# Products with w_pb in a hybrid decoder layer taken to Strassen's recursion, with tiles of w_pa between its pairs

## The chip, the cores and the metric

The kernel runs on one core of a Trainium2 chip. The metric is the device time of one execution in microseconds (us). Engines: TensorE (PE) multiplies matrices, VectorE (DVE), ScalarE (ACT) and GpSimd (POOL) do the element-wise work, SyncE (SP) issues most loads. Each engine runs its instructions in order; semaphores order them against one another.

## What is computed

One decoder layer, in float32, on 576 tokens (512 of a prompt and 64 of a sample), with model width 1024:

```python
h      = x @ w_in          # u | v | q | k | v | gate_A | gate_B
y_A    = u * (tril(W_s[g]) v_chunk + b_s[g])          # chunked spatial gating
y_B    = sliding-window attention with sinks
m      = (sigmoid(gate_A) * (y_A @ w_pa) + sigmoid(gate_B) * (y_B @ w_pb)) @ w_o
x      = LN1(alpha * x + m);  x = LN2(alpha * x + SwiGLU(x))
```

The change concerns the gates (16 column tiles of w_in, 128 columns each), y_A @ w_pa and y_B @ w_pb (8 column tiles each).

## The kernel before

**Numbers.** Every float32 operand is split into a high part (a cast on ScalarE, line 115) and a low part (a subtraction on VectorE, line 116). A product is three matmuls: high by high, high by low, low by high. Weights come as units of 512 KB in the order in which the host packed them (`_weights`). `fetch` loads a unit into one of three `raw` buffers, `convert` splits it into `hi` and `lo` (four buffers each). Names ending in h or hi, l or lo are the two parts.

**Two ways to multiply.** `fm` takes one column tile of 128 weights: 8 pieces of the inner dimension by 2 halves of the tokens (288 each) by 3, so 48 matmuls. `pair` takes two column tiles at once by Strassen's recursion in Winograd's form: seven products (B11, T1, T2, B22, B21, T3, T4) of 12 matmuls, 84 instead of 96, into three PSUM banks x, y, z, whose contents are added in the output tiles g and u on VectorE (line 225) or copied there by ScalarE (lines 228, 231, 238). Its weights are sums of the quarters of two units, made in `weight_group`: "sums" (two subtractions on VectorE, one on GpSimd), "1" (split of B11 and T1), "2" (T3 and T2, from the tile t), "3" (B22, B21, and a subtraction on GpSimd), "4" (T4). While a pair multiplies, the next pair's weights are made; a pair's last product T4 runs inside the next pair, after its T1. The left operands need sums of the quarters of the activations: for the input x these are S1, S2, S4 (`input_sums`, made during the products of v, acc_v, from loads xr) and S3 (`input_sum3`, made at the start of the gates from four more loads xs and written over a part of X).

**Stages around the change.** acc_v (v, ends at 259.0 us); seven gate pairs (to 359.3), during which steps of other work, the list `todo` (layer norm of v, key outputs, spatial gate, splits of y_A), are taken up at two spots of each pair; eight w_pa tiles by `fm`, whose results are multiplied by sigmoid(gate) (`times`, line 987); eight w_pb tiles by `fm`, each followed by `times`, an addition on GpSimd (line 1003) and a split of the sum into the stacked operand m (`stacked`, lines 1010 to 1013); the output projection acc_o. The feed-forward part after it uses `pair` throughout.

**What sets the order.** Inside a `manual_schedule` the engines' order is the program's order; elsewhere a scheduler chooses it from modelled costs. SG is a pool of four buffers of 128x576, C and R are pools of larger tiles that are handed on when their last reader is done.

Of the kernel before, what the change touches and what calls it, by code (L numbers as in the profile page):

```python
# [18 lines left out]
P = 128  # L19
# [58 lines left out]
class Builder:  # L78
# [135 lines left out]
    def pair(self, name, left, g, u, first, final, more):  # L214
# [8 lines left out]
        nxt = self.weight_group() if more else self.units_ahead()  # L223
# [5 lines left out]
        self.spare(0)  # L229
        go(z, "T1")  # L230
        nc.scalar.copy(out=u[:, hi], in_=z)
        nxt["1"]()
        if rest:
            rest()
        w["4"]()
        self.spare(2)
        go(x, "T2", False)
        nc.scalar.copy(out=u[:, lo], in_=x)
        self.spare(3)
        go(z, "B22", False)  # L240
        add(u, lo, z)
        go(y, "B21")
        add(g, lo, y)
        first()
        nxt["3"]()
        go(x, "T3", False)
        add(u, hi, x)
        nxt["2"]()

        def finish():  # L250
            go(x, "T4", False)
            final(x)

        self.rest, self.w = finish, nxt
# [5 lines left out]
    @staticmethod  # L260
    def left(x, S):

        out = {
            "B11": lambda c: (x[:, c, :HB], x[:, c, NT : NT + HB]),
            "B21": lambda c: (x[:, 4 + c, :HB], x[:, 4 + c, NT : NT + HB]),
            "T4": lambda c: (x[:, 4 + c, HB:NT], x[:, 4 + c, NT + HB :]),
        }
        for n, (hi, lo) in zip(("T1", "T2", "T3", "B22"), S):
            out[n] = lambda c, hi=hi, lo=lo: (hi[:, c], lo[:, c])
        return out  # L270
# [619 lines left out]
    def input_sums(self):  # L890

        nc = self.nc
        S = [[self.C([4, HB], F32R, f"X{n}{i}") for i in "hl"] for n in ("S1", "S2", "S4")]
        tt = lambda e, out, x, y, op: e.tensor_tensor(out=out, in0=x, in1=y, op=op)
        for c in range(4):
            p, q = self.SG(f"xr{c}"), self.SG(f"xr{c + 4}")
            nc.sync.dma_start(out=p[:], in_=self.I["xT"][:, c])
            nc.sync.dma_start(out=q[:], in_=self.I["xT"][:, c + 4])
            a11, a21, a12, a22 = p[:, :HB], p[:, HB:], q[:, :HB], q[:, HB:]
            tt(nc.gpsimd, a22, a21, a22, ALU.add)  # L900
            tt(nc.vector, a11, a22, a11, ALU.subtract)
            tt(nc.vector, a12, a12, a11, ALU.subtract)
            for (hi, lo), a in zip(S, (a22, a11, a12)):
                self.split(hi[:, c], lo[:, c], a)
        self.XSums = S

    def input_sum3(self):

        nc = self.nc
# [27 lines left out]
    def merge(self):  # L937
# [22 lines left out]
        self.todo.insert(4, self.key_outputs)  # L960
# [16 lines left out]
        for g in range(len(yA), 8):  # L977
            part(yA, self.u[g // 2][:, g % 2], self.C, f"yA{g}")

        def product(j, name, y):  # L980
            ps = [self.bank(f"ps{name}{j}_{b}") for b in range(2)]
            self.fm(ps, self.unit(KC), lambda k: (y[k][:, 0], y[k][:, 1]))
            return ps

        def times(ps, x, out):
            for b, t0, t1 in HALVES:
                nc.vector.tensor_tensor(out=out[:, t0:t1], in0=ps[b][:, :HB], in1=x[:, t0:t1], op=ALU.mult)

        for j in range(8):
            ps = product(j, "pa", yA)  # L990
            with self.tc.issue_after(self.last_split.ins):
                times(ps, T[j], T[j])
# [3 lines left out]
        for j in range(8):  # L996
            part(yB, self.yB[j // 2][:, j % 2], self.C, f"yBs{j}")
        self.m = []
        for j in range(8):
# [98 lines left out]
    def ffn(self):  # L1098
# [26 lines left out]
        self.spots = (3,)  # L1125
# [135 lines left out]
def _weights(w_in, w_pa, w_pb, w_o, w_gate, w_up, w_down):  # L1261
# [30 lines left out]
    for w in (w_pa, w_pb):  # L1292
        for j in range(8):
            fm(w[:, P * j : P * j + P])
# [70 lines left out]
```

## Time and profile before

| | |
|---|---|
| three runs | 909.65, 911.98 and 2240.95 us, median 911.98 |
| profiled execution | 911.2 us, span 909.5 |
| TensorE busy | 886.5 us, 97% of the span |
| VectorE, ScalarE, GpSimd busy | 608.1, 388.5, 164.5 us |
| granted TensorE clock | 0.991 on average |

A share of the span is an average over stages. Where an engine that is busy 97% of the time waits, its waits are few and can be listed one by one, each with the instruction that ended it. The line numbers in the profile are those of the kernel before; a helper's line (283 for every matmul, 115 and 116 for every split) stands for many places, so the tile's name tells which one is meant, with buffer numbers left out.

### The profile page before, as it was taken

Reading aid. Unit: us, or ns where it says so; the run is one execution under the profiler, and the core shown is the slowest. Engines: PE = TensorE matmul, PEld = TensorE weight load, DVE = VectorE, ACT = ScalarE, POOL = GpSimd, SP = SyncE. Lnnn points to the kernel's source line nnn. Section 1 sums busy time; section 2 is a strip of 40 time slices with the busy share of each in tenths; the row PEclk is TensorE's granted clock in tenths of the full one; section 3 lists DMA queues with packets and bytes.
Section 4 is the critical chain, followed back from the end, with each engine's and each line's share of the span. In section 5 each row is a group of like instructions: output and inputs, shape, how many; then the busy total and the mean of one; then the engine's idle time right before and its main releaser. Section 6 shows DMA issues by size and latency. Waiting matters only on the chain.

```text
span 909.5 us, 14732 instructions
## 1 busy us (share of the span) xinstructions
PE 886.5 (97%) x5963; PEld 830.5 (91%) x5963; DVE 608.1 (67%) x893; ACT 388.5 (43%) x739; POOL 164.5 (18%) x190
## 2 busy tenths in 40 slices
PE   9799999999998999999999999999999999999996
PEld 7799999997888999999988999999999998888885
DVE  4578977865677779245657877777777779315146
ACT  4456665566245447122231444444444457211110
POOL 1003123332242210002201222222222210000003
PEclk9899999999999999999999999999999999999998
DMA  7731212426131324444261012233222225322202
GB/s 210 209 102 47 71 48 75 157 94 221 47 108 63 111 94 138 155 131 140 74 227 47 1 50 91 97 100 99 98 94 95 93 94 157 101 90 82 81 1 105
DMA packets 33101, 93.16 MB, mean 102 GB/s; under 512 B 4039, under 2 KB 11095, under 8 KB 33001
## 3 DMA queue, kind: packets, MB, share of 16 engines
q1 hardware_dynamic: 32840, 90.04, 30.7%
q10 hardware_dynamic: 192, 2.18, 0.6%
q8 instruction: 47, 0.77, 0.3%
q14 instruction: 22, 0.17, 0.1%
HBM read 88.08 MB, written 6.10 MB: 104 GB/s over the span
## 4 chain that ended last, share of the span: by engine, by line
PE 78%; DVE 11%; ACT 5%; DMA 3%; issue 2%; POOL 1%; SPq 0%; POOLq 0%; ACTq 0%; DVEq 0%
PE d L283 15%; PE xf L283 14%; PE zf L283 7%; PE acc_o L283 6%; PE pspb L283 6%; PE pspa L283 6%; PE acc_v L283 5%; PE xg L283 4%; PE yf L283 3%; DMA raw<-in_wall_dram 3%; PE ffn L283 3%; ACT work L563 2%; PE zg L283 2%; DVE lo L116 2%; PE psg L283 1%
## 5 line engine op out<-in xcount | busy, mean ns | idle before, releaser
L116 DVE TENSOR_TENSOR lo<-raw,hi 128x1024 fp32r<-128x1024 f32 (+1 forms) x86 | 108.6, 1271 | 106.5 <-ACT hi L115 106.1
L115 ACT CAST hi<-raw 128x1024 fp32r<-128x1024 f32 (+1 forms) x86 | 84.1, 990 | 180.1 <-PE d L283 82.6
L116 DVE TENSOR_TENSOR glo<-raw,ghi 128x1024 fp32r<-128x1024 f32 (+1 forms) x81 | 87.5, 1081 | 65.0 <-ACT ghi L115 64.5
L283 PE MATMUL d<-hi,h 128*128 128x512 f32 (+1 forms) x440 | 128.0, 368 | 0.0
L115 ACT CAST ghi<-raw 128x1024 fp32r<-128x1024 f32 (+1 forms) x81 | 72.6, 898 | 52.6 <-DVE raw L178 42.0
L283 PEld LDWEIGHTS d<-hi,h 128*128 128x128 f32 x440 | 79.8, 188 | 13.8
L283 PE MATMUL d<-lo,h 128*128 128x512 f32 (+1 forms) x242 | 89.6, 370 | 0.0
L178 POOL TENSOR_TENSOR raw<-raw,t 128x512 f32<-128x512 f32 x27 | 34.9, 1292 | 177.4 <-DVE glo L116 165.2
L283 PE MATMUL xf<-x1T,ghi 128*128 128x288 f32 x320 | 65.0, 295 | 0.0
L116 DVE TENSOR_TENSOR glo<-t,ghi 128x1024 fp32r<-128x1024 f32 x27 | 58.1, 2153 | 0.0
L178 POOL TENSOR_TENSOR t<-raw,raw 128x512 f32<-128x512 f32 x27 | 35.9, 1329 | 100.5 <-DVE raw L178 100.5
L283 PEld LDWEIGHTS d<-lo,h 128*128 128x128 f32 x242 | 45.6, 188 | 7.8
L283 PEld LDWEIGHTS xf<-x1T,ghi 128*128 128x128 f32 x320 | 51.4, 188 | 0.2 <-DVE u L225 0.2
L283 PE MATMUL xf<-x1T,glo 128*128 128x288 f32 x160 | 47.1, 294 | 0.0
L283 PE MATMUL acc_o<-hi,m 128*128 128x512 f32 x144 | 46.2, 390 | 0.0
L313 POOL TENSOR_SCALAR lnr<-lnmv 128x1 f32<-128x1 f32 (+1 forms) x15 | 13.6, 907 | 175.8 <-DVE lnmv L331 172.6
L283 PE MATMUL psu<-X,hi 128*128 128x288 f32 x256 | 44.1, 294 | 0.0
L283 PE MATMUL pspb<-yBs,hi 128*128 128x288 f32 x256 | 44.1, 293 | 0.0
L283 PE MATMUL pspa<-yA,hi 128*128 128x288 f32 x256 | 44.1, 294 | 0.0
L283 PE MATMUL acc_v<-hi,X 128*128 128x512 f32 x128 | 41.6, 391 | 0.0
L563 ACT ACTIVATE work<-work,att 128x128 f32<-128x128 f32 x64 | 25.0, 391 | 37.6 <-DVE att L560 37.6
L283 PE MATMUL psq<-X,hi 128*128 128x288 f32 x224 | 38.6, 294 | 0.0
(339 smaller groups left out, 2402.8 us busy)
## 6 DMA issues: line engine op xcount, KB each, us to landing
raw<-in_wall_dram SPq DMA_DIRECT2D x133, 512.0 KB
xr<-in_xT_dram SPq DMA_DIRECT2D x8, 288.0 KB
z<-in_xtok_dram SPq DMA_DIRECT2D x4, 512.0 KB
xraw<-in_xT_dram SPq DMA_DIRECT2D x3, 576.0 KB
out_y_prompt_dram<-z SPq DMA_DIRECT2D x3, 512.0 KB
xs<-in_xT_dram SPq DMA_DIRECT2D x4, 288.0 KB
circ<-bout SPq DMA_DIRECT2D x1, 1024.0 KB
Bsel<-circ SPq DMA_DIRECT2D x2, 512.0 KB
```

What stands on the lines that cost most here:

```text
L115: self.nc.scalar.copy(out=hi, in_=src)
L116: return self.nc.vector.tensor_tensor(out=lo, in0=src, in1=hi.bitcast(F32), op=ALU.subtract)
L178: sub = lambda e, out, x, y: e.tensor_tensor(out=out, in0=x, in1=y, op=ALU.subtract)
L283: self.last_mm = self.nc.tensor.matmul(out, l, r, start=start, stop=stop, **more)
L313: self.nc.gpsimd.tensor_scalar_add(r[:n], mv[:n, 1:2], EPS)
L563: nc.scalar.activation(out=pr[:, r], in_=sel[:, r], func=AF.Exp, bias=nm[:, r : r + 1], accum_out=rs[:, r : r + 1])
```

## The change

1. **w_pb.** The products with w_pb become four Strassen pairs (p0 to p3). Their left operands are splits of y_B (tile Y, in the buffer of X) and of its sums (SA, SB), which are made between the first w_pa tiles, partly on GpSimd. The first five w_pa tiles run plainly, the other three stand between a pair's T3 and T4. Multiplying by the gates (`final`), adding the w_pa part on GpSimd and stacking m move into the pairs. The host packs w_pb's units as sums ask for them.
2. **S3 of the input.** The difference a11 - a21 is formed on GpSimd inside `input_sums`, when the loads xr are there, and kept in two SG tiles (s3_0, s3_1) until the gates start; the loads xs go. Two of the four SG buffers are left for the eight xr tiles.
3. **Side work.** The two spots of a gate pair are now directly after the next pair's "sums" (0, 6) instead of before T2 and B22 (2, 3); `pair` takes its steps from a table `plan`.

```diff
+        if plan is None:
+            nxt = self.weight_group() if more else self.units_ahead()
+            plan = {0: (nxt["sums"],), 2: (nxt["1"],), 3: (w["4"],), 6: (nxt["3"],), 7: (nxt["2"],)}
         go = lambda out, n, first=True: self.product(out, w["ops"][n], left[n], first, True)
         add = lambda t, s, ps: nc.vector.tensor_tensor(out=t[:, s], in0=ps, in1=t[:, s], op=ALU.add)
-        nxt["sums"]()
+
+        def do(n):
+            if n in (6, 7):
+                self.spare(n)
+            for step in plan.get(n, ()):
+                step()
+            if n not in (6, 7):
+                self.spare(n)
+
+        do(0)
...
+        s3 = [self.SG(f"s3_{i}") for i in range(2)]
+        self.s3raw = [s3[c // 2][:, HB * (c % 2) : HB * (c % 2) + HB] for c in range(4)]
...
+            tt(nc.gpsimd, self.s3raw[c], a11, a21, ALU.subtract)
...
-            p = self.SG(f"xs{c}")
-            nc.sync.dma_start(out=p[:], in_=self.I["xT"][:, c])
-            nc.gpsimd.tensor_tensor(out=p[:, HB:], in0=p[:, :HB], in1=p[:, HB:], op=ALU.subtract)
-            self.split(hi[:, c], lo[:, c], p[:, HB:])
+            self.split(hi[:, c], lo[:, c], self.s3raw[c])
...
-        self.spots = (2, 3)
+        self.spots = (0, 6)
...
+        def sums(c):
+
+            p, q = (self.yB[k // 2][:, k % 2] for k in (c, c + 4))
+            self.split(Y[:, c, :HB], Y[:, c, NT : NT + HB], p[:, :HB])
+            self.split(Y[:, c + 4, :NT], Y[:, c + 4, NT:], q)
+            a11, a21, a12, a22 = p[:, :HB], p[:, HB:], q[:, :HB], q[:, HB:]
+            tt = lambda e, out, x, y, op: e.tensor_tensor(out=out, in0=x, in1=y, op=op)
+            tt(nc.gpsimd, a22, a21, a22, ALU.add)
+            tt(nc.gpsimd, a21, a11, a21, ALU.subtract)
+            tt(nc.vector, a11, a22, a11, ALU.subtract)
+            tt(nc.vector, a12, a12, a11, ALU.subtract)
+            part(SA, p, self.C, f"SA{c}")
+            part(SB, q, self.C, f"SB{c}")
...
+        plain = 5
+        for j in range(plain):
+            u = self.unit(KC, ahead=int(j + 1 < plain))
+            if j + 1 == plain:
+                self.first_pair()
+            ps = product(j, u)
             with self.tc.issue_after(self.last_split.ins):
-                times(ps, T[j], T[j])
+                times(j, ps)
+            if j < 4:
+                sums(j)
...
+        half = lambda t, s: lambda c: (t[c][:, 0, s], t[c][:, 1, s])
+        lo, hi = slice(0, HB), slice(HB, NT)
+        left = self.left(Y, (half(SB, hi), half(SA, lo), half(SA, hi), half(SB, lo)))
         self.m = []
-        for j in range(8):
-            ps = product(j, "pb", yB)
-            with self.tc.issue_after(self.last_split.ins):
-                times(ps, gB[j], gB[j])
-            nc.gpsimd.tensor_tensor(out=gB[j][:], in0=gB[j][:], in1=T[j], op=ALU.add)
-            self.m.append(self.stacked(gB[j], f"m{j}"))
+        stack = lambda: self.m.append(self.stacked(gB[len(self.m)], f"m{len(self.m)}"))
+
+        def pairs(i):
+
+            j = 2 * i
+            r = self.C([2, NT], F32, f"pb{i}")
+            g, u = r[:, 0], r[:, 1]
+            ga, gb = gB[j], gB[j + 1]
+            mul = lambda out, x, y: nc.vector.tensor_tensor(out=out, in0=x, in1=y, op=ALU.mult)
+
+            def final(x):
+                mul(ga[:, hi], x, ga[:, hi])
+                mul(gb[:], u, gb[:])
+                for k, t in ((j, ga), (j + 1, gb)):
+                    nc.gpsimd.tensor_tensor(out=t[:], in0=t[:], in1=T[k], op=ALU.add)
+
+            w = self.w
+            n = self.unit_no
+            follows = i < 3
+            nxt = []
+            one = lambda: self.convert(len(self.pieces))
+            if follows:
+                self.unit_no += 1
+
+                def begin():
+                    nxt.append(self.weight_group())
+                    nxt[0]["sums"]()
+                    nxt[0]["1"]()
+
+                late, last = begin, lambda: nxt[0]["3"]()
+            else:
+                late, last = one, one
+            stacks = (stack,) if i else ()
+            plan = {0: (w["2"],) if i else (), 2: (one,), 3: (w["4"],), 6: (late,) + stacks, 7: (last,) + stacks}
+            self.pair(f"p{i}", left, g, u, lambda: mul(ga[:, lo], g[:, lo], ga[:, lo]), final, plan=plan)
+            if follows:
+                self.w = nxt[0]
+                f = lambda t: t.rearrange("p (a b) -> p a b", a=KC)
+                ps = product(plain + i, tuple(f(t) for t in self.pieces[n]))
+                self.end_pairs()
+                times(plain + i, ps)
+
+        with self.tc.manual_schedule():
+            for i in range(4):
+                pairs(i)
+        self.end_pairs()
+        while len(self.m) < 8:
+            stack()
...
-    for w in (w_pa, w_pb):
-        for j in range(8):
-            fm(w[:, P * j : P * j + P])
+    col = lambda w, j: w[:, P * j : P * j + P]
+    for j in range(5):
+        fm(col(w_pa, j))
+    for i in range(4):
+        pair(col(w_pb, 2 * i), col(w_pb, 2 * i + 1))
+        if i < 3:
+            fm(col(w_pa, 5 + i))
```

**Place 1: VectorE at the start of the gates.** glo30 and glo32 are the low parts of the weights of pairs 0 and 1, X<-xs the splits of S3, v and lnst layer norm, T0<-zg, yg, xg the additions of pair 0. Before:

```order
L116 TENSOR_TENSOR glo32_0_2947<-raw32_2897,ghi32_0_2946 128x1024
L116 TENSOR_TENSOR X_101<-xs1_2874,X_101 128x288
L116 TENSOR_TENSOR X_101<-xs2_2879,X_101 128x288
L116 TENSOR_TENSOR X_101<-xs3_2884,X_101 128x288
L116 TENSOR_TENSOR glo30_6_2953<-raw31_2707,ghi30_6_2952 128x512
L331 BN_AGGR lnmv_2864<-lnst_2683 128x2
L331 BN_AGGR lnmv_2866<-lnst_2689 64x2
L336 SCALAR_TENSOR_TENSOR v3_2418<-v3_2418,lnmv_2864,lnvg_2395 128x1024
L225 TENSOR_TENSOR T0_2910<-zg0_2913,T0_2910 128x288
L225 TENSOR_TENSOR T0_2910<-yg0_2912,T0_2910 128x288
L116 TENSOR_TENSOR glo32_2_3006<-raw33_2914,ghi32_2_3005 128x1024
L225 TENSOR_TENSOR T0_2910<-xg0_2911,T0_2910 128x288
```

Now:

```order
L333 BN_STATS lnst_2695<-v4_2419 64x6
L344 BN_AGGR lnmv_2870<-lnst_2689 128x2
L344 BN_AGGR lnmv_2872<-lnst_2695 64x2
L116 TENSOR_TENSOR glo32_0_2947<-raw32_2891,ghi32_0_2946 128x1024
L116 TENSOR_TENSOR glo30_6_2953<-raw31_2713,ghi30_6_2952 128x512
L227 TENSOR_TENSOR T0_2904<-zg0_2907,T0_2904 128x288
L227 TENSOR_TENSOR T0_2904<-yg0_2906,T0_2904 128x288
L349 SCALAR_TENSOR_TENSOR v3_2418<-v3_2418,lnmv_2870,lnvg_2395 128x1024
L116 TENSOR_TENSOR glo32_2_3000<-raw33_2908,ghi32_2_2999 128x1024
L227 TENSOR_TENSOR T0_2904<-xg0_2905,T0_2904 128x288
```

The splits of S3 have left the place (they stand before glo30 now), and the layer-norm step L349 (L336 before), which stood ahead of T0<-zg, comes after T0<-yg.

**Place 2: TensorE where the first w_pa tile meets the last product (T4, weights ghi42_6) of the last gate pair.** Names pspa with two numbers are a column tile's banks, yA are the left operands. Before:

```order
L283 MATMUL pspa0_1_3907<-yA4_3894,hi44_3758 128x288 x2
L283 MATMUL pspa0_0_3906<-yA4_3894,lo44_3759 128x288
L283 MATMUL pspa0_1_3907<-yA4_3894,lo44_3759 128x288
L283 MATMUL pspa0_0_3906<-yA5_3897,hi44_3758 128x288 x2
L283 MATMUL pspa0_1_3907<-yA5_3897,hi44_3758 128x288 x2
L283 MATMUL xg6_3727<-X_101,ghi42_6_3776 128x288 x2
L283 MATMUL xg6_3727<-X_101,glo42_6_3777 128x288
```

Now:

```order
L296 MATMUL pspa0_0_3901<-yA0_3838,lo44_3775 128x288
L296 MATMUL pspa0_1_3902<-yA0_3838,lo44_3775 128x288
L296 MATMUL pspa1_0_3967<-yA0_3838,hi45_3841 128x288 x2
L296 MATMUL pspa1_1_3968<-yA0_3838,hi45_3841 128x288 x2
L296 MATMUL pspa2_0_4039<-yA0_3838,hi46_3860 128x288 x2
L296 MATMUL pspa2_1_4040<-yA0_3838,hi46_3860 128x288
L296 MATMUL pspa1_0_3967<-yA0_3838,lo45_3842 128x288
L296 MATMUL pspa1_1_3968<-yA0_3838,lo45_3842 128x288
L296 MATMUL pspa0_0_3901<-yA1_3865,hi44_3774 128x288
L296 MATMUL xg6_3732<-X_101,ghi42_6_3792 128x288 x2
L296 MATMUL xg6_3732<-X_101,glo42_6_3793 128x288
```

Before, 34 matmuls on yA0 to yA5 stood ahead of T4; now 15 on yA0 (of three column tiles) and one on yA1.

**Place 3: VectorE between two pairs of w_pb.** pb0<-xp0 is the addition of pair 0's T3, gb3_0 and gb3_1 the multiplications by the gates (`final`, after T4), pspa5 the w_pa tile between them, glo52_4 the low part of T3 and T2 of pair 1. The program before had here:

```order
L116 TENSOR_TENSOR lo55_4515<-raw55_4386,hi55_4514 128x1024
L987 TENSOR_TENSOR gb3_0_3292<-pspb0_0_4384,gb3_0_3292 128x288
L987 TENSOR_TENSOR gb3_0_3292<-pspb0_1_4385,gb3_0_3292 128x288
L116 TENSOR_TENSOR lo56_4578<-raw56_4449,hi56_4577 128x1024
L1011 TENSOR_TENSOR m0_4443<-gb3_0_3292,m0_4443 128x512
L1013 TENSOR_TENSOR m0_4443<-gb3_0_3292,m0_4443 128x64
```

Now:

```order
L227 TENSOR_TENSOR pb0_4252<-xp0_4253,pb0_4252 128x288
L116 TENSOR_TENSOR glo52_2_4358<-raw53_4284,ghi52_2_4357 128x1024
L1044 TENSOR_TENSOR gb3_0_3297<-xp0_4253,gb3_0_3297 128x288
L1044 TENSOR_TENSOR gb3_1_3298<-pb0_4252,gb3_1_3298 128x576
L1016 TENSOR_TENSOR T1_3021<-pspa5_0_4362,T1_3021 128x288
L1016 TENSOR_TENSOR T1_3021<-pspa5_1_4363,T1_3021 128x288
L116 TENSOR_TENSOR glo52_4_4435<-t52_4336,ghi52_4_4434 128x1024
L116 TENSOR_TENSOR lo54_4469<-raw54_4294,hi54_4468 128x1024
```

Before, a split of the unit after the next stood behind each tile's multiplications; now the split glo52_4, which pair 1 multiplies by in its third product, stands behind four multiplications that wait for T4 and the w_pa tile.

## Rows read from the trace of the kernel before

**Rows 1.** The profile page: length, busy time of each engine, and the shares of the chain of waits that ended last.

```profile
span 909.5 us, 14732 instructions
...
PE 886.5 (97%) x5963; PEld 830.5 (91%) x5963; DVE 608.1 (67%) x893; ACT 388.5 (43%) x739; POOL 164.5 (18%) x190
...
PE 78%; DVE 11%; ACT 5%; DMA 3%; issue 2%; POOL 1%; SPq 0%; POOLq 0%; ACTq 0%; DVEq 0%
```

**Rows 2.** What TensorE (PE) waited for between 200 and 560 us; columns: line waited for, us in total, times, longest.

```profile
PE xg L283 <- DVE T L225: 2.7, 2, 1.5
PE zg L283 <- ACT T L231: 1.8, 1, 1.8
```

**Rows 3.** Busy time in stretches of the span: length, then for each engine us busy and (x) instructions, the granted clock of TensorE, DMA share and GB/s. In order: the first two gate pairs; the products with w_pa; the pairs of the feed-forward part.

```profile
259.00:289.00 30.00, 25.51 (x186) 24.62 (x185) 22.34 (x31) 15.33 (x28) 12.06 (x13) 1.00 0.34 114
352.00:406.00 54.00, 54.00 (x413) 54.00 (x412) 26.24 (x41) 16.79 (x22) 0.00 (x0) 1.00 0.38 128
537.00:759.00 222.00, 221.99 (x1669) 221.54 (x1668) 168.20 (x208) 108.80 (x187) 50.49 (x39) 1.00 0.29 97
```

**Rows 4.** The chain of waits from 340 to 460 us: start, us, what. The first two rows are the first matmuls on w_pa and the last product of the last gate pair.

```profile
353.22 4.48 PE pspa L283 x34
357.71 1.60 PE xg L283 x12
...
405.50 50.43 PE pspb L283 x383
```

**Rows 5.** TensorE at the gate start: start, us, operation, and in brackets the idle time before it with what ended it. The row at 259.00 is the first matmul of the first pair; 288.25 begins the last product of the second pair.

```profile
259.00 0.42 PE L283 MATMUL xg<-X,ghi 128*128 128x288 f32 x2
...
265.71 0.40 PE L283 MATMUL zg<-XS4h,ghi 128*128 128x288 f32 x1 [1.77 <-ACT T L231]
...
275.45 0.54 PE L283 MATMUL xg<-X,ghi 128*128 128x288 f32 x2 [1.53 <-DVE T L225]
...
288.25 0.54 PE L283 MATMUL xg<-X,ghi 128*128 128x288 f32 x2 [1.19 <-DVE T L225]
```

**Rows 6.** What stood before those waits, same columns: SyncE's queue, GpSimd (POOL), ScalarE (ACT) and VectorE (DVE).

```profile
256.70 6.50 SPq L913 DMA_DIRECT2D xs<-in_xT_dram  x4
...
264.10 3.29 POOL L914 TENSOR_TENSOR xs<-xs 128x288 f32<-128x288 f32 x4
...
264.92 0.43 ACT L115 CAST X<-xs 128x288 fp32r<-128x288 f32 x1 [2.07 <-POOL xs L914]
265.26 0.39 ACT L231 COPY T<-zg 128x288 f32<-128x288 f32 x1
...
268.40 1.18 DVE L116 TENSOR_TENSOR X<-xs,X 128x288 fp32r<-128x288 f32 x3
...
281.96 1.28 DVE L338 SCALAR_TENSOR_TENSOR v<-v,lnr,lnvb 128x1024 f32<-128x1024 f32 x1
...
287.75 0.45 DVE L225 TENSOR_TENSOR T<-xg,T 128x288 f32<-128x288 f32 x1
```

**Rows 7.** VectorE and GpSimd in the products with w_pb, and VectorE in two pairs of the feed-forward part.

```profile
408.22 1.23 DVE L116 TENSOR_TENSOR lo<-raw,hi 128x1024 fp32r<-128x1024 f32 x1 [1.98 <-ACT hi L115]
411.59 0.82 DVE L987 TENSOR_TENSOR gb<-pspb,gb 128x288 f32<-128x288 f32 x2 [2.15 <-PE pspb L283]
412.55 2.46 DVE L116 TENSOR_TENSOR lo<-raw,hi 128x1024 fp32r<-128x1024 f32 x1
...
412.49 1.43 POOL L1003 TENSOR_TENSOR gb<-gb,g 128x576 f32<-128x576 f32 x1 [69.48 <-DVE gb L987]
...
548.24 2.23 DVE L116 TENSOR_TENSOR glo<-t,ghi 128x1024 fp32r<-128x1024 f32 x1
...
554.17 0.75 DVE L1164 TENSOR_TENSOR hraw<-u,g 128x576 f32<-128x576 f32 x1
...
559.40 2.23 DVE L116 TENSOR_TENSOR glo<-t,ghi 128x1024 fp32r<-128x1024 f32 x1
```

**Rows 8.** VectorE around the start of the w_pa products.

```profile
352.38 0.44 DVE L225 TENSOR_TENSOR T<-yg,T 128x288 f32<-128x288 f32 x1
352.75 2.08 DVE L116 TENSOR_TENSOR yA<-u,yA 128x576 fp32r<-128x576 f32 x3
...
355.89 0.45 DVE L225 TENSOR_TENSOR T<-xg,T 128x288 f32<-128x288 f32 x1
```

**Rows 9.** The loads of the input and the sums made of it: SyncE's queue (SPq), GpSimd, VectorE; then the TensorE matmul that first reads the unit which VectorE splits at 234.92.

```profile
202.97 0.42 SPq L898 DMA_DIRECT2D xr<-in_xT_dram  x1
...
216.44 0.33 SPq L898 DMA_DIRECT2D xr<-in_xT_dram  x1
...
207.89 0.79 POOL L894 TENSOR_TENSOR xr<-xr,xr 128x288 f32<-128x288 f32 x1 [4.67 <-PE acc_v L283]
...
219.64 0.81 POOL L894 TENSOR_TENSOR xr<-xr,xr 128x288 f32<-128x288 f32 x1 [5.17 <-DMA xr<-in_xT_dram]
...
215.04 0.46 DVE L116 TENSOR_TENSOR XS2l<-xr,XS2h 128x288 fp32r<-128x288 f32 x1
...
226.17 0.46 DVE L116 TENSOR_TENSOR XS4l<-xr,XS4h 128x288 fp32r<-128x288 f32 x1
...
234.92 1.22 DVE L116 TENSOR_TENSOR lo<-raw,hi 128x1024 fp32r<-128x1024 f32 x1
...
237.93 0.39 PE L283 MATMUL acc_v<-lo,X 128*128 128x512 f32 x1
```

More of the change, by code (lines that the diff above doesn't have):

```diff
@@ L212, in spare, with pair @@
             self.todo.pop(0)()
-    def pair(self, name, left, g, u, first, final, more):
+    def pair(self, name, left, g, u, first, final, more=None, plan=None):
         nc = self.nc
@@ L222, in pair @@
         w, rest = self.w, self.rest
-        nxt = self.weight_group() if more else self.units_ahead()
+        if plan is None:
+            nxt = self.weight_group() if more else self.units_ahead()
+            plan = {0: (nxt["sums"],), 2: (nxt["1"],), 3: (w["4"],), 6: (nxt["3"],), 7: (nxt["2"],)}
         go = lambda out, n, first=True: self.product(out, w["ops"][n], left[n], first, True)
         add = lambda t, s, ps: nc.vector.tensor_tensor(out=t[:, s], in0=ps, in1=t[:, s], op=ALU.add)
-        nxt["sums"]()
+        def do(n):
[6 more added lines that the diff above has]
+        do(0)
         go(x, "B11")
         nc.scalar.copy(out=g[:, lo], in_=x)
-        self.spare(0)
+        do(1)
         go(z, "T1")
         nc.scalar.copy(out=u[:, hi], in_=z)
-        nxt["1"]()
+        do(2)
         if rest:
             rest()
-        w["4"]()
-        self.spare(2)
+        do(3)
         go(x, "T2", False)
         nc.scalar.copy(out=u[:, lo], in_=x)
-        self.spare(3)
+        do(4)
         go(z, "B22", False)
         add(u, lo, z)
+        do(5)
         go(y, "B21")
@@ L244, in pair @@
         first()
-        nxt["3"]()
+        do(6)
         go(x, "T3", False)
         add(u, hi, x)
-        nxt["2"]()
+        do(7)
         def finish():
@@ L252, in finish @@
             final(x)
-        self.rest, self.w = finish, nxt
+        self.rest = finish
+        if more is not None:
+            self.w = nxt
     def end_pairs(self):
@@ L267, in left @@
         }
-        for n, (hi, lo) in zip(("T1", "T2", "T3", "B22"), S):
-            out[n] = lambda c, hi=hi, lo=lo: (hi[:, c], lo[:, c])
+        for n, s in zip(("T1", "T2", "T3", "B22"), S):
+            out[n] = s if callable(s) else lambda c, s=s: (s[0][:, c], s[1][:, c])
         return out
@@ L978, in merge, with product, times @@
             part(yA, self.u[g // 2][:, g % 2], self.C, f"yA{g}")
-        def product(j, name, y):
-            ps = [self.bank(f"ps{name}{j}_{b}") for b in range(2)]
-            self.fm(ps, self.unit(KC), lambda k: (y[k][:, 0], y[k][:, 1]))
+        Y = self.px.tile([P, KC, 2 * NT], F32R, tag="x", name="Y")
+        SA, SB = [], []
+        def sums(c):
[10 more added lines that the diff above has]
+            part(SB, q, self.C, f"SB{c}")
+        def product(j, u):
+            ps = [self.bank(f"pspa{j}_{b}") for b in range(2)]
+            self.fm(ps, u, lambda k: (yA[k][:, 0], yA[k][:, 1]))
             return ps
-        def times(ps, x, out):
+        def times(j, ps):
             for b, t0, t1 in HALVES:
-                nc.vector.tensor_tensor(out=out[:, t0:t1], in0=ps[b][:, :HB], in1=x[:, t0:t1], op=ALU.mult)
-        for j in range(8):
-            ps = product(j, "pa", yA)
+                nc.vector.tensor_tensor(
+                    out=T[j][:, t0:t1], in0=ps[b][:, :HB], in1=T[j][:, t0:t1], op=ALU.mult)
+        plain = 5
[4 more added lines that the diff above has]
+            ps = product(j, u)
             with self.tc.issue_after(self.last_split.ins):
-                times(ps, T[j], T[j])
+                times(j, ps)
+            if j < 4:
+                sums(j)
         with self.tc.issue_after(self.copied.ins):
@@ L1291, in _weights @@
         pair(col(o_g, j), col(o_g, j + 1))
-    for w in (w_pa, w_pb):
-        for j in range(8):
-            fm(w[:, P * j : P * j + P])
+    col = lambda w, j: w[:, P * j : P * j + P]
[5 more added lines that the diff above has]
+            fm(col(w_pa, 5 + i))
     for i in range(2):
```

8 lines of the change are left out of this document (3 added, 5 removed).

## The prediction, on record before the changed kernel ran

> **What bounds the kernel now.** I read the page first: TensorE is busy 97% of the span and carries 78% of the chain that ended last, VectorE 67%, GpSimd 18% [rows 1]. A matmul taken away therefore counts in full as long as its place has no other bound, and a wait counts in full too. So the second view is the list of TensorE's waits in the stages of the change: three in 360 us, 4.5 us together, all in the first two gate pairs [rows 2]. The windows by stage show the same: 25.51 of 30 us busy there, no idle time in the products with w_pa nor in the feed-forward pairs, at a granted clock of 1.00 (the 2.4 GHz level) [rows 3]. Third, the chain through the merge consists of TensorE alone: 50.43 us in the w_pb products [rows 4]. Last, the timelines around each place where the change puts a new wait.
>
> All sums are against the profiled execution, 911.2 us; the median of the runs is 911.98, 0.8 higher, and the last line is put on that scale.
>
> **1. Fewer products.** Eight w_pb tiles by the plain way take 50.43 us [rows 4]. A Strassen pair is priced by the feed-forward part, where the same split of a pair's weights recurs after 559.40 - 548.24 = 11.16 us [rows 7], 1.594 for each of seven products, with TensorE busy throughout. Four pairs: 44.64. Gain **5.8**, if nothing new is late.
>
> **2. The waits at the gate start.** From the first matmul of pair 0 (259.00) to T4 of pair 1 (288.25) [rows 5] are 29.25 us. In them stand 15 products: pair 0's seven, the six of pair 1 without T4, and the first two of pair 2; 15 x 1.594 = 23.9. So 5.3 us go there: 4.49 in recorded waits (1.77, 1.53, 1.19) [rows 5], the rest in slower matmuls behind each. The first wait ends with ScalarE's copy T<-zg, which stood behind the cast X<-xs, which waited for GpSimd's xs [rows 6]: with S3 made early neither stands there. The other two end with VectorE's T<-xg, which T4 needs because it reuses bank x. VectorE was late by three splits X<-xs (1.18) and layer-norm steps of 1.28 [rows 6]; the first go to a time when VectorE is not waited for, the second behind the additions of zg and yg (place 1). Following VectorE's new order by these durations, the T<-xg additions end about 1 us ahead of T4, and a pair holds some 10.5 us of VectorE work in 12.5 us with its side work. Gain **5.3**, bounds 0 (the waits only move) and 5.3.
>
> **3. The start of w_pa.** T4 of the last gate pair had 34 matmuls (4.48 us) as cover [rows 4], now 16, some 2.1 us (place 2). VectorE's T<-xg stood behind three yA splits (2.08) and one of weights and ended at 356.34 [rows 8]; now it stands behind one yA split (0.69) and one of weights (1.22) and would end near 355.2 against T4's start at 353.22 + 2.1 = 355.3. But yA0 now sits in that queue and its buffer comes free later, so the first pspa matmul can be late itself. Bounds 0 and 2.5 (the cover lost, 4.48 - 2.1, rounded up); I take **+0.9**, a yA split with its hand-over, since T<-xg itself has little room.
>
> **4. Three transitions between pairs.** After T4 (place 3), VectorE must multiply 288 columns from PSUM, 576 from SBUF and twice 288 from PSUM, then split glo52_4, which the third product of the next pair reads with its third matmul, 3 x 1.594 + 0.27 = 5.05 us after T4's start. The durations: 0.45 (half of 0.82, rounded up), 0.75, 0.82, 1.23 [rows 7]. T4 ends at 1.6, the first multiplication starts at 1.8, the split at about 3.6, and it ends at 4.8, in time. Yet GpSimd's additions of 1.43 us are released by the same multiplications. A VectorE operation with two SBUF sources that meets one gets through only when that ends: 412.55 took 2.46 instead of 1.23, GpSimd's addition had started at 412.49 [rows 7]; the feed-forward splits glo<-t take 2.23 likewise, every time [rows 7]. Behind the rest of one addition glo52_4 ends at 5.4, behind both at 6.7. So 0.3 late each by one, 1.65 by two, 0 without a meeting; I take **+0.9** for three, since one addition is released before the split and the second only after the first has run. Bounds 0 and 5.
>
> **5. Input loads in series.** With two SG buffers left, each of the rounds after the first must wait for the last split of the round before. A load landed in 3.2 us (216.44 to GpSimd's 219.64); a bound above is 4.9 (202.97 to 207.89, where GpSimd was released by something else) [rows 9]. A round is 3.2 plus about 3.0 of adds, casts and splits, so three from 215.5 (the split at 215.04 frees the first [rows 9]) end near 234.1 instead of 226.6. Behind them on VectorE stand statistics, two weight sums and the split that ended at 236.14 before; it moves to about 238.3. TensorE reads it at 237.93 [rows 9]. **+0.4**; with 4.9 us per load, +5.5. The Trainium skill, "SBUF — State Buffer", section "The DMA setup-cost knee", gives about 2 us plus bytes over 436 GB/s, an estimate of 2.7 us for 288 KB; by it this term would be 0. The measured 3.2 decides here.
>
> **Costed at nothing.** The five plain w_pa tiles hold the sums of y_B: by the durations of rows 7 VectorE has some 27 us of work in their 31.6 us, GpSimd eight additions of 0.81 [rows 9]. If the cover goes, pair 0's weights are late (rival B). The stacking of m in the pairs takes VectorE to about 13 of 17.5 us per pair and w_pa tile, against 168.2 of 222 us in the feed-forward part, which runs without idle time on TensorE [rows 3]. Loads: three units of 512 KB per 17.5 us, 90 GB/s, where 128 GB/s went by during w_pa [rows 3]. The four xs loads (6.50 us of SyncE's queue [rows 6]) go.
>
> Sum: 911.2 - 5.8 - 5.3 + 0.9 + 0.9 + 0.4 = **902.3**; on the scale of the median **903**.
>
> **Rivals.**
> A. *No new waits*: terms 3 to 5 are covered. 911.2 - 11.1 = 900.1, median scale 901. For it: the margins I find missing are below 1 us each. Against: four places would all have to hold. Chance 0.13.
> B. *VectorE and GpSimd hold each other up.* If both additions get ahead of the split in each transition (3 x 1.35 more), or GpSimd's eight additions of 0.81 (6.5 us) come on top of VectorE's 27 us in the 31.6 us of w_pa (up to 1.9 late), the time is 904 to 908, 906 most likely. For it: glo<-t at 2.23 in each feed-forward pair [rows 7]. Against: during w_pa VectorE had 26.24 of 54 us of work [rows 3], and multiplications from PSUM are not held up (411.59 [rows 7]). The Trainium skill speaks against the change here: "Perfetto Trace Analysis", section "Optimizing Scalar/DVE Operations", warns that work handed from VectorE to GpSimd may gain nothing because they share an SBUF read port. Rows 7 show such a hold-up at 412.55, in this case as large as GpSimd's whole addition. Chance 0.22.
> C. *The gate waits only move*: GpSimd and VectorE still carry the layer-norm steps in the first two pairs, now before the next weights' splits. 902.3 + 5.3 = 907.6, median 908. For it: the two later waits are VectorE's and only part of their cause is removed. Chance 0.11.
> D. *The other side: the serial input loads.* Each landing enters three times. The other terms give 902.3 - 0.4 = 901.9; the gain is gone when 3 x (landing - 3.2) + 0.4 reaches 9.3, at 6.2 us per landing. At 6.5 us: 901.9 + 10.3 = 912.2, median 913. For it: weights are loaded at the same time, and one row allows 4.9. Against: the clean row is 3.2. Chance 0.07, most of it within 2%.
> E. *The change doesn't do what it says*: w_pb's pairs run at the plain pace, since each is surrounded by w_pa tiles and term 1 is lost to weights that come late. 902.3 + 5.8, 909 on the median scale. Against: the feed-forward pairs do it with the same weight work. Chance 0.05.
>
> **How the numbers follow.** The forecast itself, 901.5 to 905 on the median scale, has 0.42. The range from 899.5 to 909.5 takes in A, B, C and the upper bound of term 4, and leaves out D, part of E, and sums of several mishaps: about 2 in 10. A change below 2% (18 us) can hardly be told from none here, and no case reaches that far: faster by more than 2% would need 893.7, beyond all the gains named (0.02); slower by more than 2% would need 930.2, which asks for a wait that no row shows (0.03).
>
> **What would show it.** Term 1: four stretches of seven products of about 11.2 us in the w_pb part. Term 2: no waits <- T in the first two gate pairs, T4 of pair 1 near 283. Term 3: the gap before the first pspa matmul and before T4. Term 4: waits of xp <- glo in three places. Term 5: a wait of acc_v <- lo just before 238. I am wrong if TensorE's idle time between 230 and 460 us is above 4 us, or if the gate part has not become some 5 us shorter.

## The result and the profile after

The changed kernel takes 900.47 us in the median of four runs (899.93 to 901.71), the kernel before 911.98 in the median of three (909.65 to 912.87); ratio 0.9881, 95% interval [0.9855, 0.9907]. A fourth run of the kernel before, 2240.95 us, is left out of both. In a second set of runs it was 901.67 against 910.60, ratio 0.9898 [0.9881, 0.9915]. So it is about 1.1% faster, some 9 to 11.5 us. The profiled execution takes 901.71 us; its span of 900.0 is 9.5 below that of before.

The page of the changed kernel, the lines that answer to [rows 1] (in this kernel every helper's line number is larger: 296 stands for 283, 227 for 225, 242 for 231):

```profile
span 900.0 us, 14730 instructions
...
PE 880.3 (98%) x5915; PEld 824.0 (92%) x5915; DVE 632.2 (70%) x933; ACT 403.5 (45%) x767; POOL 190.9 (21%) x206
...
PE 81%; DVE 9%; ACT 4%; DMA 3%; issue 1%; POOL 1%; SPq 0%; POOLq 0%; ACTq 0%
```

```profile
PE pspa L296 <- DVE yA L116: 0.3, 1, 0.3
```

The second fence is the profile's list of TensorE's waits between 200 and 560 us, where there were 4.5 us [rows 2]. It leaves out the shortest: the timeline has three more gaps of 0.15 us between the pairs of w_pb, which come up below. TensorE lost 6.2 us of busy time, VectorE gained 24 and GpSimd 26, and still fewer waits are left.

Where the 9.5 us come from is read off three marks on TensorE's timeline: the first gate matmul (259.00 before, 258.66 after), the first w_pa matmul (353.06, 347.30) and the end of the last w_pb product (455.93, 448.42; from the latter 2.07 are taken for nine acc_o matmuls that now stand ahead of it). All stage lengths in this text are made in this way. For the changed kernel the marks are these rows:

```profile
347.30 0.53 PE L296 MATMUL pspa<-yA,hi 128*128 128x288 f32 x2
...
444.75 2.07 PE acc_o L296 x9
446.82 1.60 PE xp L296 x12
```

The first row is the first w_pa matmul in the timeline, the others are the end of the chain of waits through w_pb.

| kernel (span) | to the first gate matmul | gates | w_pa and w_pb |
|---|---|---|---|
| before (909.5) | 259.00 | 94.06 | 102.87 |
| changed (900.0) | 258.66 | 88.64 | 99.05 |
| w_pb pairs alone (905.1) | 258.57 | 94.03 | 98.90 |
| early S3 and new spots alone (905.1) | 258.69 | 89.16 | 103.60 |
| S3 as before (902.8) | 257.38 | 92.96 | 99.07 |
| spots as before (899.8) | 257.73 | 89.46 | 98.91 |

The gates gave 5.4 us, the merge (the last column) 3.8, all else 0.3. The first column scatters by itself, from 256.62 to 259.86 in the kernels below: two of TensorE's waits in the attention part, long before the change (psav and sc), differ from kernel to kernel by up to 1.5 us each. So stages are compared, rather than spans, where it comes to 1 us.

The chain of waits of the changed kernel at the gate start, against [rows 5]: TensorE alone, without a gap.

```profile
258.82 1.58 PE xg L296 x12
...
266.77 3.18 PE xg L296 x24
...
283.14 3.20 PE xg L296 x24
```

T4 of the second pair begins at 283.14; the 15 products from 258.82 take 24.32 us, of which 0.44 belong to four small matmuls of the key output that moved in: 23.88, or 1.592 each. There were 29.25.

The same chain between the first two pairs of w_pb. The first row is T4 of pair 0 (1.61 us), the row at 402.67 the rest of T2 of pair 1, from its third matmul on, the last row T4 of pair 1:

```profile
397.49 1.61 PE xp L296 x12
399.10 0.02 issue
399.12 0.04 DVE gb L1044
399.17 0.33 issue
399.50 0.75 DVE gb L1044
400.25 0.73 DVE T L1016 x2
400.98 1.65 DVE glo L116
402.63 0.04 issue
402.67 1.58 PE xp L296 x10
...
415.33 1.61 PE xp L296 x12
```

It leaves TensorE for VectorE: the two multiplications by the gate, the two of the w_pa tile, the split glo<-t. T2's first matmul stands at 402.11 in TensorE's timeline and its third was due at 402.38; it came at 402.67, and the matmuls behind it follow somewhat slower at first. From T4 to T4 it is 415.33 - 397.49 = 17.84 us, where 7 x 1.59 + 6.33 = 17.46 would do.

### The profile page after: what moved, and what is told of

Its sections match the earlier page's. It is cut to its first block, busy times and chain, and to the rows that moved or that the text cites. A ratio compares the mean times of both kernels' runs of the same rounds, so it can differ in the third digit from the quotient of the medians.

```text
span 900.0 us, 14730 instructions
## 1 busy us (share of the span) xinstructions
PE 880.3 (98%) x5915; PEld 824.0 (92%) x5915; DVE 632.2 (70%) x933; ACT 403.5 (45%) x767; POOL 190.9 (21%) x206
## 4 chain that ended last, share of the span: by engine, by line
PE 81%; DVE 9%; ACT 4%; DMA 3%; issue 1%; POOL 1%; SPq 0%; POOLq 0%; ACTq 0%
PE d L296 16%; PE xf L296 14%; PE zf L296 7%; PE acc_v L296 6%; PE pspa L296 6%; PE acc_o L296 6%; PE xg L296 5%; PE yf L296 4%; DMA raw<-in_wall_dram 3%; PE ffn L296 3%; PE zg L296 2%; PE xp L296 2%; ACT work L576 2%; PE psg L296 1%; PE psu L296 1%
## 5 line engine op out<-in xcount | busy, mean ns | idle before, releaser
L116 DVE TENSOR_TENSOR lo<-raw,hi 128x1024 fp32r<-128x1024 f32 (+1 forms) x78 | 90.6, 1169 | 108.0 <-ACT hi L115 107.0
L116 DVE TENSOR_TENSOR glo<-raw,ghi 128x1024 fp32r<-128x1024 f32 (+1 forms) x93 | 100.8, 1087 | 55.2 <-ACT ghi L115 55.2
L115 ACT CAST hi<-raw 128x1024 fp32r<-128x1024 f32 (+1 forms) x78 | 75.6, 983 | 117.8 <-PE d L296 82.6
L115 ACT CAST ghi<-raw 128x1024 fp32r<-128x1024 f32 (+1 forms) x93 | 83.3, 899 | 58.7 <-DVE raw L178 54.1
L178 POOL TENSOR_TENSOR raw<-raw,t 128x512 f32<-128x512 f32 x31 | 40.7, 1314 | 197.9 <-DVE glo L116 151.4
L178 POOL TENSOR_TENSOR t<-raw,raw 128x512 f32<-128x512 f32 x31 | 43.1, 1389 | 116.3 <-DVE raw L178 116.3
L116 DVE TENSOR_TENSOR glo<-t,ghi 128x1024 fp32r<-128x1024 f32 x31 | 64.5, 2082 | 0.0
L600 POOL TENSOR_SCALAR_AFFINE_SELECT pc<-pt 128x512 fp32r<-128x512 f32 x24 | 16.1, 672 | 112.7 <-ACT pt L115 108.4
```

The lines of the kernel that those rows point to most:

```text
L115: self.nc.scalar.copy(out=hi, in_=src)
L116: return self.nc.vector.tensor_tensor(out=lo, in0=src, in1=hi.bitcast(F32), op=ALU.subtract)
L178: sub = lambda e, out, x, y: e.tensor_tensor(out=out, in0=x, in1=y, op=ALU.subtract)
L600: nc.gpsimd.affine_select(out=f(out[:, i]), in_=f(pt[:, i].bitcast(F32)), pattern=[[0, 4], [sign, P]], compare_op=cmp, fill=0.0, base=0, c ...
```

## Experiments

**1. The parts alone.** The w_pb pairs without the rest:

```diff
-            self.split(hi[:, c], lo[:, c], self.s3raw[c])
+            p = self.SG(f"xs{c}")
+            nc.sync.dma_start(out=p[:], in_=self.I["xT"][:, c])
...
-        self.spots = (0, 6)
+        self.spots = (3, 4)
```

(Cut short: the rest of input_sums and input_sum3 is as before too, and the key outputs are again a step of their own in the side work. In the new numbering 3 and 4 are the old spots.) 

> The w_pb pairs alone: S3 again from the four loads xs at the gate start and the side work at its two old spots, all else as changed. If the terms add up, TensorE's three waits of the first two gate pairs are back (4.5 us recorded) and the profiled span is 909.5 - 3.6 = 906, the 3.6 being what the merge gained between the first w_pa matmul and the output projection in the trace of the changed kernel. Rival (the merge shortens the gates too, or the terms hang together): 902 or less.

Measured: ratio 0.9950 [0.9935, 0.9965], span 905.1. The waits, 200 to 560 us:

```profile
PE zg L296 <- ACT T L242: 1.8, 1, 1.8
PE xg L296 <- DVE T L227: 1.2, 1, 1.2
PE xp L296 <- DVE glo L116: 1.0, 4, 0.5
```

Two of the three gate waits are back by name, and the gates are as long as before (94.03). In the place of the wait that isn't back TensorE had a lower clock. Behind the wait of 1.77 us for zg the granted clock was 0.50, the 1.2 GHz level (columns as in [rows 3]):

```profile
265.48:268.89 3.41, 3.41 (x16) 3.41 (x16) 2.73 (x5) 3.39 (x7) 1.46 (x2) 0.50 0.00 0
...
274.50 0.45 DVE L227 TENSOR_TENSOR T<-xg,T 128x288 f32<-128x288 f32 x1
...
275.00 0.54 PE L296 MATMUL xg<-X,ghi 128*128 128x288 f32 x2
```

The twelve matmuls behind that wait took 2.88 us, where they took 1.70 before. It cost no time: T4 of the first pair (the last row) waits for VectorE's T<-xg, and begins 16.43 us after the first gate matmul, against 16.45 before. In the kernel before, and in the one with S3 as before, the clock stayed at 1.00 behind the same wait.

The merge keeps its gain (98.90). The third line is new. It holds the three transitions (0.15 each), and the first w_pb pair's first low part, which is 0.53 us late; that product takes 2.38 us instead of 1.58. VectorE, which makes the sums of y_B under the w_pa tiles, is late there. Why is not shown: from the first w_pa matmul to the first of w_pb it has 33.2 us here, 1 us less than in the changed kernel, but experiment 4 has 33.3 without this wait.

The other half: w_pb by `product` as before and w_pb's units in plain order, S3 and spots as changed. 

> The early S3 and the new spots alone, with w_pb multiplied plainly as before. If the terms add up, no waits in the first two gate pairs and a span of 909.5 - 5.8 = 903.7; the start of w_pa as before or up to 0.8 us later. Rival (the waits only move into the later gate pairs or the merge): 906 or more.

Measured: ratio 0.9954 [0.9939, 0.9969], span 905.1. No wait is left between the gate products; 89.16 holds one of 0.5 us for yA ahead of the first w_pa matmul, and the merge, 0.7 us longer than before, another of 0.4 for the high part of a w_pa unit. The span lies between the expected 903.7 and the rival's 906: the start of w_pa costs 0.5 + 0.7 us, more than was allowed for it, but the waits don't move on into later pairs. By stages the two halves give 4.0 and 4.9 - 0.7 = 4.2 us, together 8.2 of the 9.2 that both give at once. Of the 1 us that is lacking, 0.8 is the longer first product of w_pb in the first half, which the changed kernel doesn't have; some 0.3 is the start of w_pa, where the second half loses 1.2 us and the changed kernel 0.9 (experiment 4).

**2. Which edit removed the gate waits?** input_sums and input_sum3 as before, new spots: 

> Only S3 goes back to the loads xs at the gate start; new spots and w_pb pairs stay. By the prediction's reasons the first wait (T<-zg, 1.8 us) is back and the two others in part, since VectorE has the four splits X<-xs again but not the layer-norm steps ahead of the additions: 902.3 to 904 in span. Rival S (S3 alone made the whole gain): 905.5. Rival T (the spots made it): 900 to 900.5.

Measured: ratio 0.9930 [0.9914, 0.9947], span 902.8, gates 92.96; three waits:

```profile
264.08 0.40 PE L296 MATMUL zg<-XS4h,ghi 128*128 128x288 f32 x1 [1.76 <-ACT T L242]
...
268.15 0.53 PE L296 MATMUL xg<-X,ghi 128*128 128x288 f32 x2 [0.63 <-ACT T L248]
...
273.88 0.53 PE L296 MATMUL xg<-X,ghi 128*128 128x288 f32 x2 [0.62 <-DVE T L227]
```

The first is back, as expected. The row at 273.88 is T4 of the first pair, 16.50 us after the first gate matmul (257.38), where it was 16.45 before and is 12.73 in the changed kernel: what the first pair lost is back in full, with a wait for ScalarE between. The third wait of before, 1.19 us ahead of T4 of the second pair, is not back; the expectation had it back in part. The span falls in the expected range only because the first gate matmul came 1.3 us early: the gates are 4.3 us longer than in the changed kernel, not 2.3 to 4.0 as that range has it.

The spots as before, early S3 (the last two lines of the diff in 1, and the key outputs again a step of their own): 

> Only the spots of the side work go back; the early S3 and the w_pb pairs stay. By the prediction's reasons one or two waits for T<-xg of 0.3 to 1.3 us are back: 901 to 902.5 in span. Rival S (the early S3 made the whole gain, the layer-norm steps fit into VectorE's idle time either way): 900 to 900.5, no waits in the first two gate pairs.

Measured: ratio 0.9905 [0.9891, 0.9920], gates 89.46. In the first two gate pairs one wait is left (the second line), ended by VectorE's T<-xg at 282.40, ahead of T4 of the second pair:

```profile
PE xp L296 <- DVE glo L116: 1.0, 4, 0.5
PE xg L296 <- DVE T L227: 0.6, 1, 0.6
```

So the early S3 makes 4.6 of the 5.4 us by itself, the new spots alone 1.1, and on top of the early S3 they add 0.8. By place: the early S3 ends what the first pair lost, and the wait of the second pair is ended by the new spots, in part also by the early S3. With the old spots the merge is 0.1 shorter: T4 of the last gate pair has its 34 matmuls of cover again and nothing is late at the start of w_pa, but the first w_pb pair waits 0.55. In time the kernel with the old spots can't be told from the changed one. The wait that the prediction's reasons asked for is there, so rival S falls; the span is below the expected range, as the gates lost only 0.8 us and the first gate matmul came 0.9 early. The four splits were the larger part of VectorE's lateness, but not all.

Experiments 3 to 6 were timed once each, so they are read by their traces and not by their times.

**3. The transitions.** The multiplications of the w_pa tile and the split first, then T4's:

```diff
-            plan = {0: (w["2"],) if i else (), 2: (one,), 3: (w["4"],), 6: (late,) + stacks, 7: (last,) + stacks}
+            plan = {2: (one,), 3: (w["4"],), 6: (late,) + stacks, 7: (last,) + stacks}
...
+                times(plain + i, ps)
+                self.w["2"]()
                 self.end_pairs()
-                times(plain + i, ps)
```

> Between two pairs of w_pb, VectorE splits T3 and T2 of the next pair (glo<-t) and does the multiplications of the w_pa tile before the two multiplications by the gates that wait for T4. The step from one pair's T4 to the next, 17.84 us in the changed kernel, is 7 x 1.59 + 6.33 = 17.46 if the stall there comes from what stands ahead of glo<-t. Rival (the stall comes from the weights' or the bank's release, or VectorE is short of time in the pair): 17.8 as before, or a new wait later in the pair.

Measured: T4 to T4 17.44 us, twice; merge 97.80, 1.25 less than in the changed kernel; span 898.2.

```profile
396.80 3.18 PE xp L296 x24
...
414.24 3.18 PE xp L296 x24
...
431.68 3.18 PE xp L296 x24
```

That settles the queue on VectorE as the place, not what in it takes too long. The first try at that: GpSimd's additions are written behind the next pair's T2. 

> VectorE's order stays, only GpSimd's two additions after T4 are moved behind the next pair's T2. If GpSimd holds up the split, glo<-t takes 1.22 instead of 1.72 us and ends about 4.9 us after T4's start, in time: 17.46 to 17.5 us from T4 to T4. Rival (VectorE's queue alone is the cause, GpSimd's part is small): 17.7 or more.

Measured: 17.86, glo<-t at 1.73, GpSimd's two additions at 398.23 for 4.25 us as before. Nothing else stands in GpSimd's queue there, so the additions still start when their inputs are ready: the edit moved lines, not instructions, and says nothing. The second try takes them off GpSimd:

```diff
-                for k, t in ((j, ga), (j + 1, gb)):
-                    nc.gpsimd.tensor_tensor(out=t[:], in0=t[:], in1=T[k], op=ALU.add)
+                adds.append(lambda: [nc.vector.tensor_tensor(out=t[:], in0=t[:], in1=T[k], op=ALU.add)
+                                     for k, t in ((j, ga), (j + 1, gb))])
```

(Cut short: the next pair's table calls them as its step 4, behind its T2; the last pair's are called at once.)

> GpSimd's two additions after a pair's T4 are done by VectorE, behind the next pair's splits; VectorE's queue up to glo<-t is as in the changed kernel. If GpSimd holds up the split, glo<-t takes 1.22 instead of 1.72 us, ends 4.7 us after T4's start, and T4 to T4 is 17.44 to 17.5. Rival (the queue alone is the cause): 17.8.

VectorE and GpSimd in the changed kernel, then VectorE in this one (columns: start, us, engine, line, operation):

```profile
400.17 0.81 DVE L1016 TENSOR_TENSOR T<-pspa,T 128x288 f32<-128x288 f32 x2
400.90 1.72 DVE L116 TENSOR_TENSOR glo<-t,ghi 128x1024 fp32r<-128x1024 f32 x1
...
399.66 4.24 POOL L1050 TENSOR_TENSOR gb<-gb,g 128x576 f32<-128x576 f32 x2 [1.64 <-DVE gb L1044]
```

```profile
400.63 1.21 DVE L116 TENSOR_TENSOR glo<-t,ghi 128x1024 fp32r<-128x1024 f32 x1
...
405.16 1.42 DVE L1051 TENSOR_TENSOR gb<-gb,g 128x576 f32<-128x576 f32 x2
```

In both the split starts 3.41 us after T4. Here it takes 1.21 instead of 1.72, and T4 to T4 is 414.66 - 397.22 = 17.44. GpSimd's hold-up was the cause: the split waited for the first addition, and the second addition for the split (4.24 us for two that take 1.43 each alone [rows 7]). The multiplications of the w_pa tile, which read one operand from PSUM, were not held up beside the additions (0.81 for two). VectorE does the two additions in 1.42.

**4. The start of w_pa.**

```diff
-            self.fm(ps, u, lambda k: (yA[k][:, 0], yA[k][:, 1]))
+            self.fm(ps, u, lambda k: (yA[k][:, 0], yA[k][:, 1]), ks=(4, 5, 6, 7, 0, 1, 2, 3), ends=(4, 3))
```

(Cut short: `ends`, a new argument of `fm`, marks the first and the last piece for the accumulation.) 

> The w_pa tiles go through the inner dimension in the order yA4 to yA7, then yA0 to yA3. If the late split of yA0 causes the loss at the start of w_pa, the matmuls begin right behind T3 of the last gate pair and T4 follows without a wait: 0.7 us less there. Rival (the additions after T3 or the weights' splits are late in any case): T4 of the last gate pair waits, and less than 0.3 us is gained.

Measured: the merge takes 98.16, 0.9 less. The w_pa matmuls follow T3 without a gap, and T4 has 21 of them as cover. Two rows of its chain and the two of the changed kernel that answer to them:

```profile
348.51 2.77 PE pspa L296 x21
351.28 1.68 PE xg L296 x12
```

```profile
347.27 0.77 DVE yA L116
348.05 0.04 issue
348.09 2.16 PE pspa L296 x14
```

In the changed kernel 16 matmuls fill the same 2.8 us ahead of T4, since the third stands until VectorE's low part of yA0 is done. The late split of yA0 was the cause. The span, 900.2, doesn't show it, since the first gate matmul came at 259.86 here, after a longer psav wait (4.6 us).

**5. The serial loads.**

```diff
             nc.sync.dma_start(out=q[:], in_=self.I["xT"][:, c + 4])
+            nc.sync.dma_start(out=p[:], in_=self.I["xT"][:, c])
+            nc.sync.dma_start(out=q[:], in_=self.I["xT"][:, c + 4])
```

> Each of the eight input loads is issued twice into the same buffer, the second after the first has landed, so a landing takes some 6 us instead of 3. If the rounds are in series with next to no room behind them, as the prediction's rival D has it, each of three rounds enters with about 3 us and TensorE waits some 8 to 10 us in acc_v for the low part of the last unit: first gate matmul at 267 to 269 instead of 258.7. Rival (there is room, the loads overlap the other work): below 262.

Measured: first gate matmul at 259.74, one wait of 1.24 us for the low part, a second of 0.24 for ScalarE's T<-xg. That is below the rival's 262, but not shown to be for its reason, and the run decides little: the scheduler, which knows of the extra loads, put the split of the last unit ahead of the fourth round (its sums run at 244 us, behind the split at 237.22). How much a slower landing would cost in the changed kernel's own order stays open; what it costs at the measured landings is in the trace of that kernel, below.

**6. GpSimd's share of the sums.** Both `tt(nc.gpsimd, ...)` of the function `sums` become `tt(nc.vector, ...)`. 

> The eight sums of y_B that GpSimd makes during the w_pa tiles go to VectorE. If GpSimd's share of them costs VectorE as much in hold-ups as it saves, VectorE's busy time from 346 to 382 us stays within 1 us of 33.4 and the first w_pb pair starts without a wait. Rival (the hold-ups are small): VectorE has 3.6 us more to do than the 36 us hold, and the first w_pb pair waits 1 us or more.

The stretch from 5.7 us after the first w_pa matmul to the first w_pb pair, of the changed kernel and of this one (columns as in [rows 3]):

```profile
353.00:381.50 28.50, 28.50 (x217) 28.37 (x216) 27.18 (x39) 12.98 (x21) 9.57 (x10) 1.00 0.37 135
```

```profile
351.00:379.20 28.20, 28.20 (x217) 28.20 (x216) 25.40 (x47) 12.76 (x21) 2.06 (x2) 1.00 0.39 144
```

VectorE does eight more instructions and is busy 1.8 us less. Over the stretch that the expectation named (346 to 382 us, here 344 to 380) it is 31.91 against 33.37, 1.5 less where 1 was allowed: GpSimd's share costs VectorE more than it saves. One group of each shows why:

```profile
L116 DVE TENSOR_TENSOR Y<-yB,Y 128x576 fp32r<-128x576 f32 x4 | 4.2, 1054 | 0.0
```

```profile
L116 DVE TENSOR_TENSOR Y<-yB,Y 128x576 fp32r<-128x576 f32 x4 | 3.0, 749 | 0.0
```

The same split takes 749 ns alone and 1054 beside GpSimd. The first w_pb pair waits in neither kernel, so no time is gained there, but there is room. (Its span of 897.8 comes from a first gate matmul at 256.62.)

**7. Both losses mended.** The changes of 3 (split first) and 4 in one kernel, and the changed kernel beside it, in the same set of runs. 

> The changed kernel once more, unedited, on the chip of the next three runs, so that they are compared with it: 0.988 to 0.991 of the kernel before; a span of 899 to 901.

> The split glo<-t first between the pairs and the order yA4 to yA7, yA0 to yA3 in the w_pa tiles, both at once. If the two losses are separate, 1.2 and 0.8 us come off: 2.0 us from the first gate matmul to the last w_pb product, and 0.2% less time than the changed kernel. Rival (VectorE, now the nearest bound in the w_pa stretch, turns the second gain into a wait before the first w_pb pair): 1.2 us or less.

Measured: the changed kernel 901.67 us, ratio 0.9898 [0.9881, 0.9915], span 899.8; the mended one 899.38, ratio 0.9877 [0.9862, 0.9892], span 898.0. From the first gate matmul to the end of the last w_pb product it takes 187.71 us against 189.66: 1.95 less, as expected, and no wait of TensorE is recorded on the way. In time the medians differ by 0.25% the same way, but the intervals overlap. The mended kernel is better by its trace and not shown to be by its time.

## Why the prediction was right, point by point

It forecast 903 us, in 899.5 to 909.5, within 2%; the medians are 900.5 and 901.7. The sum for the profiled execution, 902.3, met 901.71. The profiled execution is the slowest of its four runs, though: the first median lies below the band of the forecast itself (901.5 to 905) and next to rival A's 901, the second just inside the band. The time alone can't tell the two apart; the terms can:

1. *Fewer products, -5.8.* Without stalls (the run with additions on VectorE) the four pairs take 446.88 - 381.37 less three w_pa tiles (18.99) and 2.07: 44.45 us against the 50.43 of [rows 4], -6.0.
2. *Gate start, -5.3.* -5.4, no wait left. The size was right; of the reasons, the early S3 carried most (4.6 alone) and the order of the layer-norm steps 0.8. The prediction named both for the two later waits and left the shares open.
3. *Start of w_pa, +0.9.* +0.9 by the run that removes it, by the split of yA0, as worked out. The wait stands ahead of the third w_pa matmul (348.09), not of the first or of T4, where the prediction looked for it.
4. *Transitions, +0.9.* Three times 0.38, +1.15. The mechanism was the named one: behind one GpSimd addition, not two. The sign that it named, xp <- glo in three places, is there with gaps so short (0.15) that the list of waits omits them. One of its reasons was misread: the row at 411.59 can't show that multiplications from PSUM aren't held up, as GpSimd began only at 412.49; the row at 400.17 above does show it.
5. *Serial loads, +0.4.* 0: the three rounds ended at 233.3, forecast 234.1, and the last unit's split came in time to 0.1 us, 0.9 us ahead of the forecast:

```profile
213.67 0.33 SPq L913 DMA_DIRECT2D xr<-in_xT_dram  x1
...
217.75 0.80 POOL L909 TENSOR_TENSOR xr<-xr,xr 128x288 f32<-128x288 f32 x1 [4.74 <-DMA xr<-in_xT_dram]
...
220.97 0.81 POOL L909 TENSOR_TENSOR s<-xr 128x288 f32<-128x288 f32 x1 [2.42 <-DVE XS4l L116]
...
225.81 0.33 SPq L912 DMA_DIRECT2D xr<-in_xT_dram  x1
...
228.66 1.12 POOL L909 TENSOR_TENSOR s<-xr 128x288 f32<-128x288 f32 x1 [4.63 <-DMA xr<-in_xT_dram]
...
236.18 1.22 DVE L116 TENSOR_TENSOR lo<-raw,hi 128x1024 fp32r<-128x1024 f32 x1
...
237.48 0.47 PE L296 MATMUL acc_v<-lo,X 128*128 128x512 f32 x1
```

The three landings, from issue to GpSimd's start, are 4.08, 2.91 (220.31 to 223.22) and 2.85 us, 3.28 on average: the measured 3.2 was a fair price. The Trainium skill's estimate of 2.7 us ("SBUF — State Buffer", "The DMA setup-cost knee") is near the two later ones alone. By it the term was 0, as it came out, but not by shorter landings: the rounds together took 19.6 us, forecast 18.6. What made it 0 is that they began at 213.67 instead of 215.5. The second tile of S3 took its buffer only at 220.97, when a split of the second round released it; until then three buffers and not two served the loads, so one load of each of the next two rounds was issued ahead of need (202.51 and 214.65).

So terms 1, 2 and 5 came out 0.7 us better than forecast and term 4 0.25 worse, which makes some 0.45 of the 0.6 us by which the sum was off. Another 0.3 came ahead of the gates, in the part that scatters, and the merge gained 3.8 where terms 1, 3 and 4 as measured make 4.0. That the sum met the trace to 0.6 us is in part luck; the mechanisms of terms 1 to 4 were those named.

The rivals: A (no new waits) came near in time, 900.1 against 901.7, for the wrong reason, as two of the three losses are there. B was half present: GpSimd and VectorE do hold each other up, in the transitions and under the w_pa tiles, where VectorE was busy 27.18 of 28.50 us, but the second place cost TensorE nothing in the changed kernel. With the old spots the first w_pb product is 0.8 us longer; whether the hold-up makes it so wasn't tried. C, that the gate waits only move, fell by the gates of 88.64 us. D wasn't tried cleanly. E fell by term 1.

## What to carry to other kernels

Price a wait by TensorE's products between two marks rather than by the recorded idle time: at the gate start 4.5 us were recorded and 5.4 came back, since matmuls behind a wait are slower too. And a wait can hide: in the w_pb pairs alone a lower clock stood in the place of one, and the length of the stage was the same. An addition handed to GpSimd isn't free for VectorE when both read two SBUF operands at the same time; where VectorE is near its limit, count what the hold-up adds before handing it over. Before reading an experiment that moves lines, look whether the engine's order moved.

## What the runs showed of the hardware

Eight additions of 288 columns on GpSimd cost VectorE more than it needs to do them itself (8 x 0.45 = 3.6 us). By the busy times it is some 5.4 us: 27.18 against 25.40 less the 3.6. Counted by instruction, seven of VectorE's took 0.6 us longer each beside them, 4.3 us; an eighth, a subtraction of weights (1.29 instead of 0.68), stood beside a weight subtraction of GpSimd. The Trainium skill ("SBUF — State Buffer", section "Who interferes with whom") calls the ports that the two engines share an exclusive lock, and says that a VectorE instruction with two inputs in SBUF contends with a GpSimd instruction that reads SBUF; the alternation in the transitions, addition, split, addition, agrees with it, and so do the multiplications with one input from PSUM, which kept their time. That the bill can come out against GpSimd in a stretch where it had little else to do (2.6 us) we had not expected.
